# Wider output blocks, an early part of the second block, and a residual on one engine, in a two-layer decoder on one core

## The chip, the cores and the metric

One Trainium2 chip (trn2), one NeuronCore of it. The metric is the device time of one execution in microseconds (us), the lower the better. The engines go by the names of the profile: PE is TensorE (matrix products), DVE VectorE, ACT ScalarE, POOL GpSimd, SP SyncE, whose queue issues the weight loads.

## What is computed

Two layers of a decoder over 256 positions of width 2048, in float32. Each layer has three parts, each normalised before and after and added to the residual stream `h`:

```python
h = h + rms_norm(einsum('bsc,cd->bsd', mix, w_out[l]), mix_post_g[l])
xa = memory_attention(rms_norm(h, x_pre_g[l]), rms_norm(mem, mem_g[l]), x_wq[l], x_wkv[l], x_wo[l])
h = h + rms_norm(xa, x_post_g[l])
ff = swiglu(rms_norm(h, f_pre_g[l]), f_w_gu[l], f_w_down[l])
h = h + rms_norm(ff, f_post_g[l])
```

`mix` (2048 columns, 16 chunks of 128) joins three groups of heads: differential attention (chunks 0 to 5), a sparse attention (6 to 11) and a gated product along the positions (12 to 15). Their closing product is w_out. The cross-attention over 256 memory positions closes with x_wo (4 chunks), the feed-forward network (5632 hidden columns, in two halves of 22 chunks) with w_down.

## The kernel before

**Products.** A weight is used once. `loaded` fetches it on SP's queue into one of three `raw` tiles (128 x 2048, 1 MB), `splits` makes of each 1024 columns a rounded part `hi` (ACT, line 206) and the rest `lo` (DVE, line 207), and each chunk is used in three products: rounded by rounded, rounded by rest, rest by rounded. There are three `hi` and three `lo` tiles, so PE can be three tiles behind the split at most. Two loops use them. `mm_t` holds the weights and moves 256 positions of `x`. `mm_n` (line 399) holds 128 positions of its input and moves `cols` columns of the weights; its input goes by its tile's name in the rows, `mx` (the mix), `cx` (cross-attention) or `hx` (the hidden columns), so that `acc<-hi,hx` is a closing product of the feed-forward. Per chunk it makes two `hi` and one `lo` product for each of two row tiles. `acc` has four banks, and each call of `mm_n` takes two.

**The closing products.** `TAIL` (line 259) lists the column blocks of w_out, x_wo and both halves of w_down: three of 512 and two of 256. The first half's result is copied to `og`, the second half's added to it. `project_out` (line 648) empties each block: a square on ACT with a row sum (`sqj`), and the product with the gain, on DVE or, where the second half is added, on POOL (line 681). For the last block the gain's product is held back (`rest`).

**The order at w_out.** The first block takes its chunks in the order of `MIX_FIRST`: 8 to 11, 0 to 3, 6 and 7, then 4 and 5, 12 to 15. The generators `b_heads`, `a_heads` and `chunks` split the chunks of `mix` when they are there; the first eight lie in the tiles `m6`, as `mx` is not free yet (in orders of instructions these tiles are `m_` and a number). The chain that ends last is that of the third pair of heads: transposes `oat`, scaling (`MX`), split (`mx`) for chunks 4 and 5; and the gate: `yp` on PE, a sum on DVE (`y`), POOL's product into `MX`, split for 12 to 15. `turn_memory` waits for these and then fetches and splits the memory for the cross-attention.

**The residual.** `residual` (line 585) sums the squares, forms the row factor on DVE (`rs_v`, `rs_r`, ...), adds to `H`, transposes `H` (`xtp`) and splits it for the next products. Behind x_wo and at the change of layer nothing else is there for PE to do (`bare`), so 38 `warm` products stand in between. Behind w_out the product `t_k` (names `mh`, `ml`: memory) runs meanwhile; there the last eight chunks are added as `beside`: scaled on ACT (line 601) and added on POOL (line 602). `begin` fixes the order of DVE and ACT as written during the first steps; else the program's scheduler places the instructions. `last_residual` (line 689) ends the kernel: `hsum` adds three pieces on PE, DVE five, and each goes out by DMA.

Of the kernel before, what the change touches and what calls it, by code (L numbers as in the profile page):

```python
# [58 lines left out]
def trunk(ctx: ExitStack, tc, a, onehot, out):  # L59
# [17 lines left out]
    nc.gpsimd.memset(pc.tile([P, 8], F32, name="half_pc"), 0.0)  # L77
# [181 lines left out]
    TAIL = ((0, 512), (512, 512), (1024, 512), (1536, 256), (1792, 256))  # L259
    MIX_FIRST = ((8, 4), (0, 4), (6, 2), (4, 2), (12, 4))  # L260

    def plan():
# [7 lines left out]
        for l in range(L):  # L270
# [25 lines left out]
            for i, (c0, n) in enumerate(TAIL):  # L296
                yield spec(rows(w_out, c0, n), KD, n, MIX_FIRST if i == 0 else None)
# [101 lines left out]
    def mm_n(nk, cols, xh, xl, hold=False):  # L399

        xh, xl = ([x[:, k, :] for k in range(nk)] if not isinstance(x, list) else x for x in (xh, xl))
        tiles = [acc.tile([P, 512], F32, tag="acc", name="acc") for _ in range(2)]
        for n, k, hi, lo in weights(nk, cols, hold):
            for t in range(2):
                o = tiles[t][:, :cols]
                h, lw = xh[k][:, t * P:(t + 1) * P], xl[k][:, t * P:(t + 1) * P]
                mm(o, h, hi, n == 0, False)
                mm(o, h, lo, False, False)
                mm(o, lw, hi, False, n == nk - 1)
        return tiles  # L410
# [174 lines left out]
    def residual(og, ss, evac, nxt, res, bare, off):  # L585
# [11 lines left out]
        def add(c, n, beside=False):  # L597
            f = slice(c * P, (c + n) * P)
            for t in range(2):
                if beside:  # L600
                    nc.scalar.activation(og[:, t, f], og[:, t, f], AF.Copy, scale=r[:, t:t + 1])
                    nc.gpsimd.tensor_tensor(H[:, t, f], H[:, t, f], og[:, t, f], op=ALU.add)
                else:
                    nc.vector.scalar_tensor_tensor(H[:, t, f], og[:, t, f], r[:, t:t + 1], H[:, t, f],  # L604
                                                   op0=ALU.mult, op1=ALU.add)
# [3 lines left out]


# [6 lines left out]
        if bare:  # L617
            prefetch()
# [6 lines left out]
        add(8, 4, not bare)  # L625
# [4 lines left out]
        add(12, 4, not bare)  # L630
# [17 lines left out]
    def project_out(nk, xh, xl, og, gain, add=False, first=None):  # L648
# [4 lines left out]
        for g, (c0, cols) in enumerate(TAIL):  # L653
# [6 lines left out]
            tiles = mm_n(nk, cols, *(first if first and g == 0 else (xh, xl)), hold=last)  # L660

            def evac(tiles=tiles, g=g, c0=c0, cols=cols, gb=gb, last=last):
                for t in range(2):
                    d, p = og[:, t, c0:c0 + cols], tiles[t][:, :cols]
                    if add:
                        nc.vector.tensor_tensor(d, p, d, op=ALU.add)
                        square(d, ss[:, t, g:g + 1])
                        if not last:
                            nc.gpsimd.tensor_tensor(d, d, gb, op=ALU.mult)
                    else:  # L670
                        square(p, ss[:, t, g:g + 1])
                        if not last:
                            nc.vector.tensor_tensor(d, p, gb, op=ALU.mult)
                if not last:
                    return

                def rest():
                    for t in range(2):
                        d, p = og[:, t, c0:c0 + cols], tiles[t][:, :cols]
                        if add:  # L680
                            nc.gpsimd.tensor_tensor(d, d, gb, op=ALU.mult)
                        else:
                            nc.vector.tensor_tensor(d, p, gb, op=ALU.mult)
                return rest
# [4 lines left out]
    def last_residual(og, ss, evac):  # L689
# [599 lines left out]
```

## Time and profile before

| | us |
|---|---|
| median of three runs (lowest, highest) | 2424.31 (2423.04, 2426.93) |
| the profiled execution | 2425.12 |
| its span, first to last instruction | 2423.4 |
| PE busy | 2389.2 (99%) |
| DVE busy | 1412.6 (58%) |
| ACT busy | 1188.7 (49%) |
| POOL busy | 201.9 (8%) |
| weights and inputs read | 444.72 MB |

The mean granted clock of PE over the span is 0.997 of full. Where PE is busy nearly all the time, the shares of the others say little by themselves; what is to be read is what a product costs, and the few stretches where PE waits or its clock is lower.

### The profile page before, as it was taken

The numbers are of one execution on the slowest core, as the hardware profiler recorded it, in microseconds if no ns is written. First come the engines' busy times: TensorE is split into PE (matmuls) and PEld (weight loads), VectorE is DVE, ScalarE is ACT, GpSimd is POOL, SyncE is SP. The second block draws the span as 40 slices with busy tenths as digits, with TensorE's granted clock in tenths as the row PEclk, the third lists the DMA queues.
The fourth block names the chain that finished last, engine by engine and source line by source line (L and its number), as shares of the span: only waits on it lengthen the run. The fifth ranks groups of instructions, "written<-read, shape, count | busy, mean of one in ns | idle before, by whom it ended". The sixth has DMA issues, their size and how long they took to land.

```text
span 2423.4 us, 42616 instructions
## 1 busy us (share of the span) xinstructions
PE 2389.2 (99%) x17741; PEld 2249.2 (93%) x17741; DVE 1412.6 (58%) x2129; ACT 1188.7 (49%) x1764; POOL 201.9 (8%) x177
## 2 busy tenths in 40 slices
PE   9999999999999999999999999999999999999998
PEld 8899789999998999998999997999999989999987
DVE  5686766665554455555466767666655544555554
ACT  5655545554444444444455655455544444444443
POOL 0010131000000000000100102100000000000001
PEclk9999999999999999999999999999999999999999
DMA  7755475455655565555554555644555555555553
GB/s 250 242 170 157 164 252 176 157 176 196 197 195 194 187 195 193 192 192 192 190 173 132 187 156 189 219 157 157 190 194 192 191 192 190 192 195 196 193 191 131
DMA packets 356757, 453.27 MB, mean 187 GB/s; under 512 B 11290, under 2 KB 275412, under 8 KB 356052
## 3 DMA queue, kind: packets, MB, share of 16 engines
q1 hardware_dynamic: 354836, 443.45, 55.9%
q0 software_dynamic: 1248, 6.29, 0.8%
q8 instruction: 139, 2.28, 0.4%
q10 hardware_dynamic: 480, 0.80, 0.1%
q14 instruction: 54, 0.44, 0.1%
HBM read 444.72 MB, written 5.79 MB: 186 GB/s over the span
## 4 chain that ended last, share of the span: by engine, by line
PE 91%; DVE 4%; ACT 2%; DMA 2%; issue 1%; SPq 0%; POOL 0%; ACTq 0%; POOLq 0%; DVEq 0%
PE acc L201 86%; DVE lo L207 2%; ACT hi L206 1%; PE xtp L564 1%; PE ixp L201 1%; ACT sqj L550 1%; PE lga L201 1%; DMA m<-in_mem_dram 1%; DVE H L604 1%; DMA H<-in_x_dram 0%; DVE mx L207 0%; PE warm L416 0%; DMA lp<-in_a_lambda_dram 0%; PE pvb L201 0%; PE lgx L201 0%
## 5 line engine op out<-in xcount | busy, mean ns | idle before, releaser
L207 DVE TENSOR_TENSOR lo<-raw,hi 128x1024 fp32r<-128x1024 f32 (+2 forms) x839 | 1000.9, 1194 | 870.7 <-ACT hi L206 868.4
L206 ACT ACTIVATE hi<-raw 128x1024 fp32r<-128x1024 f32 (+2 forms) x839 | 861.0, 1027 | 1037.7 <-PE acc L201 954.7
L201 PE MATMUL acc<-x,hi 128*128 128x256 f32 (+1 forms) x7360 | 1270.0, 277 | 0.0
L201 PEld LDWEIGHTS acc<-x,hi 128*128 128x128 f32 (+1 forms) x7360 | 1111.2, 188 | 2.8 <-issue 2.7
L201 PE MATMUL acc<-x,lo 128*128 128x256 f32 x3680 | 889.5, 278 | 6.8 <-DVE lo L207 4.6
L201 PEld LDWEIGHTS acc<-x,lo 128*128 128x128 f32 x3680 | 690.1, 188 | 13.4 <-DVE lo L207 6.1
L201 PE MATMUL acc<-hi,hx 128*128 128x512 f32 (+1 forms) x1760 | 452.6, 347 | 0.0
L201 PEld LDWEIGHTS acc<-hi,hx 128*128 128x128 f32 x1760 | 308.5, 189 | 41.7 <-issue 0.2
L201 PE MATMUL acc<-lo,hx 128*128 128x512 f32 (+1 forms) x880 | 304.9, 347 | 0.0
L201 PEld LDWEIGHTS acc<-lo,hx 128*128 128x128 f32 x880 | 166.7, 189 | 20.5 <-issue 0.2
L1243 POOL TENSOR_TENSOR g<-g,u 128x512 f32<-128x512 f32 x44 | 76.6, 1741 | 1131.3 <-ACT g L1241 1131.3
L201 PE MATMUL acc<-hi,mx 128*128 128x512 f32 (+1 forms) x576 | 148.1, 345 | 7.9 <-DVE mx L207 4.0
L201 PEld LDWEIGHTS acc<-hi,mx 128*128 128x128 f32 x576 | 99.6, 190 | 21.8 <-DVE mx L207 5.1
L201 PE MATMUL acc<-hi,x 128*128 128x384 f32 (+1 forms) x384 | 109.3, 360 | 0.0
L201 PE MATMUL acc<-lo,mx 128*128 128x512 f32 (+1 forms) x288 | 98.4, 343 | 0.1
L201 PEld LDWEIGHTS acc<-hi,x 128*128 128x128 f32 x384 | 70.1, 188 | 8.3 <-issue 3.3
L201 PE MATMUL acc<-lo,x 128*128 128x384 f32 (+1 forms) x192 | 69.7, 363 | 0.0
L212 ACT ACTIVATE x<-xtp,gT 128x256 fp32r<-128x256 f32 x96 | 39.5, 470 | 48.7 <-PE xtp L564 48.7
L201 PEld LDWEIGHTS acc<-lo,mx 128*128 128x128 f32 x288 | 54.6, 190 | 7.0 <-DVE lo L207 1.0
L213 DVE SCALAR_TENSOR_TENSOR x<-xtp,gT,x 128x256 fp32r<-128x256 f32 x96 | 41.6, 478 | 16.1 <-ACT x L212 15.9
L201 PE MATMUL acc<-hi,cx 128*128 128x512 f32 (+1 forms) x160 | 42.7, 352 | 0.0
L201 PEld LDWEIGHTS acc<-lo,x 128*128 128x128 f32 x192 | 36.1, 188 | 3.9 <-issue 1.3
(247 smaller groups left out, 1878.4 us busy)
## 6 DMA issues: line engine op xcount, KB each, us to landing
raw<-in_f_w_gu_dram SPq DMA_DIRECT2D x352, 512.0 KB, 4.5
raw<-in_f_w_down_dram SPq DMA_DIRECT2D x76, 1024.0 KB, 5.1
raw<-in_w_out_dram SPq DMA_DIRECT2D x30, 1024.0 KB, 5.4
raw<-in_w_in_dram SPq DMA_DIRECT2D x48, 512.0 KB, 4.7
raw<-in_w_in_dram SPq DMA_DIRECT2D x23, 1024.0 KB, 5.3
raw<-in_x_wkv_dram SPq DMA_DIRECT2D x16, 1024.0 KB, 4.9
raw<-in_w_in_dram SPq DMA_DIRECT2D x12, 960.0 KB, 5.1
raw<-in_x_wq_dram SPq DMA_DIRECT2D x8, 1024.0 KB, 5.2
```

The lines of the kernel that those rows point to most:

```text
L201: return nc.tensor.matmul(o, lhsT=lhsT, rhs=rhs, start=start, stop=stop, skip_group_check=True)
L206: nc.scalar.activation(hi, src, AF.Copy)
L207: eng.tensor_tensor(lo, src, hi.bitcast(F32), op=ALU.subtract)
L212: nc.scalar.activation(hi, src, AF.Copy, scale=scale)
L213: nc.vector.scalar_tensor_tensor(lo, src, scale, hi.bitcast(F32), op0=ALU.mult, op1=ALU.subtract)
L550: nc.scalar.activation(q[:, :src.shape[-1]], src, AF.Square, accum_out=red)
L564: nc.tensor.transpose(p[:, t * P:(t + 1) * P], src[:, t, (c + j) * P:(c + j + 1) * P], ident)
L604: nc.vector.scalar_tensor_tensor(H[:, t, f], og[:, t, f], r[:, t:t + 1], H[:, t, f], op0=ALU.mult, op1=ALU.add)
L1243: nc.gpsimd.tensor_tensor(g, g, u, op=ALU.mult)
```

## The change

The blocks of `TAIL` become four of 512. The first two blocks of w_out are cut into an early part (ten chunks) and a late one (six): both early parts come first, then both late ones, each pair of `acc` banks kept in between (`more`, `into`). In a last block the last two chunks go tile by tile. The residual behind w_out makes all its additions on DVE, and `rest` is on DVE everywhere. `last_residual` gets 24 `warm` products between its two rounds of `hsum`, and the first half's closing product is followed by `warm(2)`. `turn_memory` starts one weight later. Two paddings move tiles: `cx` starts 64 bytes earlier, which puts it at 416 past a multiple of 512 bytes, as `hx` and `mx` are (it was at 480); the one in `pc` keeps the others where they were.

```diff
-    TAIL = ((0, 512), (512, 512), (1024, 512), (1536, 256), (1792, 256))
-    MIX_FIRST = ((8, 4), (0, 4), (6, 2), (4, 2), (12, 4))
+    TAIL = ((0, 512), (512, 512), (1024, 512), (1536, 512))
+
+    MIX_EARLY, MIX_LATE = ((8, 4), (0, 4), (6, 2)), ((4, 2), (12, 4))
...
+            for part, n in ((MIX_EARLY, 10), (MIX_LATE, 6)):
+                for c0, cols in TAIL[:2]:
+                    yield spec(rows(w_out, c0, cols), n, cols, part)
+            for c0, cols in TAIL[2:]:
+                yield spec(rows(w_out, c0, cols), KD, cols)
...
+    def mm_n(nk, cols, xh, xl, hold=False, into=None, more=False):
...
+        tiles = into or [acc.tile([P, 512], F32, tag="acc", name="acc") for _ in range(2)]
...
+        for w in weights(nk, cols, hold):
+            if hold and w[0] >= nk - 2:
+                end.append(w)
+                if w[0] < nk - 1:
+                    continue
+                for t in range(2):
+                    for w in end:
+                        step(t, *w)
...
+        if not bare:
+            add(0, 2)
+            turn(0)
+            add(2, 2)
+            rest()
+            yield
+            turn(2)
+            for c in range(4, KD, 2):
+                add(c, 2)
+                yield
+                turn(c)
+            yield
+            yield from pre_norm(res)
+            return
...
+                return lambda: [scaled(t, nc.vector) for t in range(2)]
...
+        warm(24)
         dg = spread(r)
-        rest()
...
-        at = used[0]
+        at = used[0] + 1
...
-            while used[0] == at or any(g.__name__ in ("last_heads", "chunks") for g in side):
+            while used[0] <= at or any(g.__name__ in ("last_heads", "chunks") for g in side):
...
+        early = [mm_n(10, cols, *first, more=True) for _, cols in TAIL[:2]]
+        oss, evac = project_out(KD, mxx[:, 0], mxx[:, 1], og, a["mix_post_g"][l], early=early)
...
-        cx = kp.tile([P, 2080], F32R, name="cx")[:, 32:].rearrange("p (a h t) -> p a h t", a=2, h=4)
+        cx = kp.tile([P, 2064], F32R, name="cx")[:, 16:].rearrange("p (a h t) -> p a h t", a=2, h=4)
...
+                warm(2)
```

The order on PE at the start of w_out, layer 0, as it was (from the last products of chunk 7 to the first of the `yp`):

```order
L201 MATMUL acc<-lo,mx 128x512
L201 MATMUL acc<-hi,mx 128x512
L1014 MATMUL oat<-ident,o_3079 128x128 x4
L201 MATMUL acc<-hi,mx 128x512
L201 MATMUL acc<-lo,mx 128x512
L201 MATMUL acc<-hi,mx 128x512
L201 MATMUL acc<-lo,mx 128x512
L201 MATMUL yp<-wsT,vg 128x128 x2
L201 MATMUL acc<-hi,mx 128x512 x3
L201 MATMUL acc<-lo,mx 128x512
L201 MATMUL acc<-hi,mx 128x512 x2
```

Behind the ten early chunks stood `oat`, and directly behind that the products that need its split. Now, from the same place:

```order
L201 MATMUL acc<-lo,mx 128x512
L201 MATMUL acc<-hi,mx 128x512
L201 MATMUL acc<-hi,m_2366 128x512 x2
L201 MATMUL acc<-lo,m_2366 128x512
L201 MATMUL acc<-hi,m_2366 128x512
L201 MATMUL acc<-lo,m_2366 128x512
L201 MATMUL acc<-hi,m_2366 128x512 x2
L201 MATMUL acc<-lo,m_2366 128x512
L201 MATMUL acc<-hi,m_2366 128x512 x2
L201 MATMUL acc<-lo,m_2366 128x512
L201 MATMUL acc<-hi,m_2366 128x512
L201 MATMUL acc<-hi,m_2367 128x512
L1040 MATMUL oat<-ident,o_3079 128x128 x4
```

and further on, where block 1's early part ends and the late part of block 0 begins:

```order
L201 MATMUL acc<-lo,m_2366 128x512
L201 MATMUL acc<-hi,m_2367 128x512
L201 MATMUL acc<-hi,mx 128x512
L201 MATMUL acc<-lo,mx 128x512
L201 MATMUL acc<-hi,mx 128x512 x2
L201 MATMUL yp<-wsT,vg 128x128 x4
L201 MATMUL acc<-lo,mx 128x512
L201 MATMUL acc<-hi,mx 128x512 x2
```

The tiles `m_` and `mx` of the early chunks are used a second time, for block 1: 60 products, with `oat` behind the 13th of them and four of the eight `yp` near their end; the other four `yp` stand four products into chunk 4.

On DVE, in the residual behind w_out of layer 0, it was:

```order
L472 SCALAR_TENSOR_TENSOR rs_u<-rs_q,rs_r 128x2
L473 SCALAR_TENSOR_TENSOR rs_r<-rs_u,rs_r 128x2
L604 SCALAR_TENSOR_TENSOR H<-og,rs_r,H 128x256 x8
L207 TENSOR_TENSOR lo<-raw,hi 128x1024 x2
L213 SCALAR_TENSOR_TENSOR x<-xtp,gT,x 128x256 x4
L207 TENSOR_TENSOR lo<-raw,hi 128x1024 x2
```

and it is now:

```order
L491 SCALAR_TENSOR_TENSOR rs_u<-rs_q,rs_r 128x2
L492 SCALAR_TENSOR_TENSOR rs_r<-rs_u,rs_r 128x2
L619 SCALAR_TENSOR_TENSOR H<-og,rs_r,H 128x256 x11
L207 TENSOR_TENSOR lo<-raw,hi 128x1024
L619 SCALAR_TENSOR_TENSOR H<-og,rs_r,H 128x256 x5
L207 TENSOR_TENSOR lo<-raw,hi 128x1024
L213 SCALAR_TENSOR_TENSOR x<-xtp,gT,x 128x256 x4
L207 TENSOR_TENSOR lo<-raw,hi 128x1024 x2
```

Eight additions of 256 columns stood ahead of the next `lo` tiles, the other half of the sum being on POOL; now there are eleven, one `lo`, and five more.

## Rows read from the trace of the kernel before

**Rows 1.** The page: engine totals (busy us, share, instructions), and the waits' chain by line

```profile
PE 2389.2 (99%) x17741; PEld 2249.2 (93%) x17741; DVE 1412.6 (58%) x2129; ACT 1188.7 (49%) x1764; POOL 201.9 (8%) x177
...
PE acc L201 86%; DVE lo L207 2%; ACT hi L206 1%; PE xtp L564 1%; PE ixp L201 1%; ACT sqj L550 1%; PE lga L201 1%; DMA m<-in_mem_dram 1%; DVE H L604 1%; DMA H<-in_x_dram 0%; DVE mx L207 0%; PE warm L416 0%; DMA lp<-in_a_lambda_dram 0%; PE pvb L201 0%; PE lgx L201 0%
```

**Rows 2.** PE by line and form: count | busy us, mean ns | idle before, releasers

```profile
L201 PE MATMUL acc<-hi,hx 128*128 128x256 f32 x704 | 127.4, 283 | 0.0
L201 PE MATMUL acc<-hi,mx 128*128 128x512 f32 x320 | 102.0, 395 | 7.9 <-DVE mx L207 4.0 <-ACT mx L206 3.9
L201 PE MATMUL acc<-hi,mx 128*128 128x256 f32 x256 | 46.4, 283 | 0.0
...
L201 PE MATMUL acc<-mh,lo 128*128 128x256 f32 x128 | 34.2, 297 | 5.4 <-DVE lo L207 5.4
L201 PE MATMUL acc<-hi,cx 128*128 128x512 f32 x96 | 31.8, 402 | 0.0
L201 PE MATMUL acc<-hi,cx 128*128 128x256 f32 x64 | 11.2, 276 | 0.0
...
L201 PE MATMUL yp<-wsT,vg 128*128 128x128 f32 x32 | 4.8, 284 | 0.6 <-DVE y L1088 0.6
```

**Rows 3.** Timeline, PE, w_down's second half, layer 0: start, us, instruction, count [idle before]

```profile
1177.58 0.39 PE L201 MATMUL acc<-lo,hx 128*128 128x512 f32 x1
...
1178.26 0.39 PE L201 MATMUL acc<-lo,hx 128*128 128x512 f32 x1
...
1180.95 0.28 PE L201 MATMUL acc<-lo,hx 128*128 128x256 f32 x1
...
1181.31 0.28 PE L201 MATMUL acc<-lo,hx 128*128 128x256 f32 x1
```

**Rows 4.** Timeline, PE, first block of w_out, layer 0

```profile
288.20 0.50 PE L201 MATMUL acc<-hi,mx 128*128 128x512 f32 x1 [1.95 <-ACT mx L206]
...
292.07 0.97 PE L201 MATMUL acc<-hi,mx 128*128 128x512 f32 x3 [2.04 <-DVE mx L207]
```

**Rows 5.** Timeline, POOL and DVE, the same stretch

```profile
287.69 3.78 POOL L1079 TENSOR_TENSOR vg<-vg,lnb 128x512 f32<-128x512 f32 x2 [122.60 <-ACT MX L1015]
...
288.04 2.31 DVE L207 TENSOR_TENSOR lo<-raw,hi 128x1024 fp32r<-128x1024 f32 x1
290.27 1.74 DVE L207 TENSOR_TENSOR mx<-MX,mx 128x512 fp32r<-128x512 f32 x1
```

**Rows 6.** Timeline: residual behind w_out, layer 0; last row, behind x_wo

```profile
378.55 7.40 DVE L604 SCALAR_TENSOR_TENSOR H<-og,rs_r,H 128x256 f32<-128x256 f32 x8
...
379.94 5.73 POOL L602 TENSOR_TENSOR H<-H,og 128x512 f32<-128x512 f32 x4 [3.60 <-ACT og L601]
...
387.23 0.55 PE L201 MATMUL acc<-mh,lo 128*128 128x256 f32 x1 [2.68 <-DVE lo L207]
...
481.59 1.67 DVE L604 SCALAR_TENSOR_TENSOR H<-og,rs_r,H 128x256 f32<-128x256 f32 x4
```

**Rows 7.** Windows: length, then busy (count) of PE, PEld, DVE, ACT, POOL; PEclk, DMA, GB/s

```profile
387.07:390.48 3.41, 3.25 (x15) 3.28 (x16) 3.41 (x7) 0.55 (x2) 0.00 (x0) 0.50 0.17 59
...
1585.15:1588.56 3.41, 2.83 (x13) 2.86 (x14) 3.41 (x7) 0.92 (x4) 0.00 (x0) 0.50 0.11 39
```

**Rows 8.** Timeline, PE: transposes behind x_wo (layer 0) and at the change of layer

```profile
482.78 1.03 PE L564 MATMUL xtp<-ident,H 128*128 128x128 f32 x8
...
1216.65 1.63 PE L564 MATMUL xtp<-ident,H 128*128 128x128 f32 x8 [0.88 <-DVE H L604]
```

**Rows 9.** The end: timeline of DVE and PE, and a window of the output's transfer

```profile
2414.69 3.40 DVE L708 SCALAR_TENSOR_TENSOR H<-og,rs_r,H 128x512 f32<-128x512 f32 x5
...
2414.92 4.34 PE L201 MATMUL hsum<-og,dg 128*128 128x512 f32 x6 [2.68 <-DVE dg L487]
...
2416.40:2421.80 5.40, 2.86 (x5) 0.86 (x3) 1.68 (x3) 1.79 (x3) 0.00 (x0) 0.82 1.01 382
```

**Rows 10.** The page: DMA issues, KB each, median us from issue to landing

```profile
raw<-in_w_out_dram SPq DMA_DIRECT2D x30, 1024.0 KB, 5.4
```

More of the change, by code (lines that the diff above doesn't have):

```diff
@@ L397, in mm_t, with step @@
         return tiles
-    def mm_n(nk, cols, xh, xl, hold=False):
+    def mm_n(nk, cols, xh, xl, hold=False, into=None, more=False):
         xh, xl = ([x[:, k, :] for k in range(nk)] if not isinstance(x, list) else x for x in (xh, xl))
[L402 to L409, printed above, removed]
+        tiles = into or [acc.tile([P, 512], F32, tag="acc", name="acc") for _ in range(2)]
+        def step(t, n, k, hi, lo):
+            o = tiles[t][:, :cols]
+            h, lw = xh[k][:, t * P:(t + 1) * P], xl[k][:, t * P:(t + 1) * P]
+            mm(o, h, hi, n == 0 and not into, False)
+            mm(o, h, lo, False, False)
+            mm(o, lw, hi, False, n == nk - 1 and not more)
+        end = []
+        for w in weights(nk, cols, hold):
[6 more added lines that the diff above has]
+                        step(t, *w)
+            else:
+                for t in range(2):
+                    step(t, *w)
         return tiles
@@ L624, in residual @@
         turn(6)
-        add(8, 4, not bare)
+        add(8, 4)
         yield
@@ L629, in residual @@
         turn(10)
-        add(12, 4, not bare)
+        add(12, 4)
         yield
@@ L646, in begin, with project_out @@
         start(gen)
-    def project_out(nk, xh, xl, og, gain, add=False, first=None):
+    def project_out(nk, xh, xl, og, gain, add=False, early=()):
         ss = sm.tile([P, 2, len(TAIL)], F32, tag="sso", name="sso", bufs=2)
@@ L659, in project_out, with scaled @@
                 nc.gpsimd.dma_start(gb, gain[c0:c0 + cols].partition_broadcast(P))
-            tiles = mm_n(nk, cols, *(first if first and g == 0 else (xh, xl)), hold=last)
+            if g < len(early):
+                tiles = mm_n(6, cols, [xh[:, k, :] for k in range(KD)], [xl[:, k, :] for k in range(KD)], into=early[g])
+            else:
+                tiles = mm_n(nk, cols, xh, xl, hold=last)
             def evac(tiles=tiles, g=g, c0=c0, cols=cols, gb=gb, last=last):
+                def scaled(t, eng):
+                    d, p = og[:, t, c0:c0 + cols], tiles[t][:, :cols]
+                    if add:
+                        eng.tensor_tensor(d, d, gb, op=ALU.mult)
+                    else:
+                        nc.vector.tensor_tensor(d, p, gb, op=ALU.mult)
                 for t in range(2):
@@ L666, in evac @@
                         nc.vector.tensor_tensor(d, p, d, op=ALU.add)
[L667 to L684, printed above, removed]
+                    square(d if add else p, ss[:, t, g:g + 1])
+                    if not last:
+                        scaled(t, nc.gpsimd)
+                return lambda: [scaled(t, nc.vector) for t in range(2)]
             if last:
@@ L703, in last_residual @@
             t, f = pieces[i]
+            if i == 2:
+                rest()
             p = summed.get((t, f.start))
```

18 lines of the change are left out of this document (5 added, 13 removed).

## Prediction

> **What bounds the kernel now.** I read the engine totals and the chain of waits first. TensorE is busy 99% of the span, and 86% of the chain that ended last is `acc` products of line 201 [rows 1]. So the time is a count of matmuls times their spacing, plus the few places where TensorE stands still or runs at half clock; work on other engines matters only there. I then grouped TensorE's rows by form (how many products of which width, and the idle time ahead of them, [rows 2]), took the spacing from a stretch where wide and narrow blocks meet [rows 3], and went to each place with idle time: the start of the output projection [rows 4, 5], the residual behind it [rows 6, 7], the change of layer [rows 8] and the end [rows 9].
>
> The reader is to see three things. Three products of 512 columns start 0.68 us apart from the next three (1177.58 to 1178.26), three of 256 columns 0.36 us (1180.95 to 1181.31): 0.2267 us against 0.1200 us each [rows 3], so that two narrow ones cost 0.0133 us more than the wide one that does the same work. At the start of w_out TensorE waits 1.95 and 2.04 us for the split of a late chunk [rows 4]. Behind w_out it waits for a `lo` tile, 5.4 us in both layers together [rows 2], and then the granted clock is at 0.50, the 1.2 GHz level, for 3.41 us in each layer [rows 7].
>
> The sum is made against the profiled execution (2425.1 us, a span of 2423.4 and 1.7 around it), which lies 0.8 us above the median of the three runs. What counts as no change is 0.2%, 4.8 us.
>
> **The change, part by part.**
>
> *Blocks of 512 in place of two of 256.* In w_down the narrow form with `hx` has 704 `hi` products [rows 2] and, by the loop (one `lo` for two `hi`), 352 `lo`: 1056, or 528 pairs, at 0.0133 us: -7.0 us over both halves and both layers. In w_out (`mx`) 256 + 128 = 384, or 192 pairs, -2.6 us; the mean of a narrow `mx` product is the same 283 ns as that of `hx` [rows 2]. The cross-attention's output (`cx`) is different: its narrow products are 7 ns shorter than the others (276 against 283), its wide ones 7 ns longer than those of `mx` (402 against 395) [rows 2], so widening alone would cost 48 pairs some +0.3 us. But the change also moves `cx` by 64 bytes, to the place within 512 bytes at which `hx` and `mx` lie; if its wide products then go like theirs, 144 of them save 7 ns, -1.0 us. I take -1.0 and keep +0.3. Ten chunks of the second block now come from the `m6` tiles: 120 wide products in two layers, between 0 and 7 ns dearer by the same rows, +0.4 taken. Sum -10.2 us, between -10.6 and -8.5. No cover is needed: these rows lie on the path. Narrow and wide blocks load the same bytes, in pieces twice as long, and split them in the same 1024-column tiles.
>
> By the Trainium skill (TensorE: Matmul & The Clock Gate, Back-to-back issue gap) a warm matmul takes N/2.4 ns plus about 2.5 ns; by that a pair would save 2.5 ns and not 13.3, and the whole part about 2 us. The measured rows differ from it, and the sum goes by the rows.
>
> *Early chunks of block 1 ahead of the late chunks of block 0.* Before, the chunks whose split comes last (4, 5 and 12 to 15) stand in the first block, directly behind the others. In the new order ten chunks of the second block, 60 products at 0.2267 = 13.6 us, come between; the transposes `oat` stand 13 products into them, which leaves 47, or 10.7 us, from there to the first product of chunk 4. The split that TensorE waited for, slowed while POOL worked, ended at 292.0 (290.27 + 1.74) [rows 5]; TensorE had run dry at 286.25 (288.20 - 1.95) [rows 4], directly behind `oat`. That is 5.8 us, and 10.7 us cover it. What goes: 7.9 us ahead of `hi,mx` and 0.6 us ahead of `yp`, both layers [rows 2], 8.5 us. What is late next: chunks 12 to 15, which need the `yp` product, the DVE add, POOL's multiply and a split, behind it. The second group of `yp` stands four products into chunk 4, with 20 products (4.5 us) from there to chunk 14; I count their chain at about 4 us. I leave 0.3 us of waiting per layer: -7.9 us, between -8.5 and -4.5 (where one of the two long waits per layer returns). All four `acc` banks are held in this time; block 2 opens behind the late chunks of block 1 (36 products, 8.2 us), which is the time that DVE and ACT have to empty block 0.
>
> *The residual behind w_out.* Before, eight adds on DVE take 7.40 us, 0.92 each, with POOL's adds beside them; the same adds alone take 1.67 us for four, 0.42 each [rows 6]. The next `lo` comes behind them, and TensorE waits 2.68 us for it [rows 6]. Now eleven adds stand there, then a `lo`, then five. With POOL empty, eleven take 4.6 us: 2.8 us less than the eight did, which is the length of the wait. Then come `lo` (1.2), five adds (2.1) and `lo`: 4.5 us for two tiles that feed TensorE for 2 x 24 products, over 5 us at 0.11 each. So TensorE keeps its feed with little to spare. The bounds for an add are 0.42 and 0.92 (both rows of this kernel); I take 0.42, since the only thing that differs between them is POOL. With the wait goes what followed it, 3.41 us at half clock per layer: half of the busy time there, 3.25 and 2.83 us [rows 7], 1.6 + 1.4 = 3.0 us. In all 5.4 + 3.0 = 8.4 us; I leave 0.6 us: -7.8 us, between -8.4 and -3. ACT loses four scalings and gains nothing here.
>
> *The change of layer.* Last product, 38 warming products, transposes. Behind the cross-attention the eight transposes take 1.03 us with no wait; at the change of layer 0.88 us of idle time stand ahead, and they take 1.63 us [rows 8]: 1.5 us more. Here a `lo` stood between the last two additions and POOL multiplied beside DVE's chain; both go, and the first tile is ready six products (1.4 us) earlier, while the last addition, square and multiply are twice as wide. The multiply by the gain on DVE (two operations of up to 0.7 us) falls behind the first adds, where DVE has gaps. -1.3 us, between -1.5 and 0. At the cross-attention the warming products cover the chain already: 0.
>
> *Two warming products behind the first half.* 2 x 0.12 us per layer, on the path: +0.5 us. Nothing waits there, so they buy nothing that I see.
>
> *The end.* The 24 warming products keep TensorE busy, so that `hsum` should run at full clock: its 4.34 us [rows 9] may become 2.6. But from 2416.4 to 2421.8 the DMA engines are full (share 1.01, 382 GB/s [rows 9]) with the 2.1 MB of output. What starts that stream is the first add on DVE at 2414.69 [rows 9], not `hsum`. The two gain multiplies go to DVE ahead of that add, and POOL is out of the way: one costs about 0.68 us (an add of 512 columns, 3.40 / 5 [rows 9]), the other saves about as much. 0, between -1 and +0.7.
>
> **Sum:** -10.2 - 7.9 - 7.8 - 1.3 + 0.5 + 0 = -26.7 us. From the median: 2424.3 - 26.7 = 2397.6 us.
>
> **The rivals.**
>
> 1. *The adds still starve TensorE.* Sixteen adds in one row on DVE leave two `lo` tiles late by as much as before, and the clock falls again. For it: DVE is busy all through the stretch, and the margin is a few tenths of a us. Against: 0.42 us alone. The 7.8 us are lost: 2405.4 us. At 0.92 each it would be worse (eleven adds 10.2 us, a wait of 5.4 us): 2411. Chance 0.13.
>
> 2. *Wide blocks win nothing.* For it: `cx`, where one wide product takes two narrow ones. Against: the direct rows of `hx` [rows 3]. All 10.2 us are lost: 2407.8 us. Chance 0.05. The rule of the Trainium skill (TensorE: Matmul & The Clock Gate) given above comes near this rival.
>
> 3. *The first wait only moves* (the change doesn't do what it says): chunks 12 to 15 come as late against their new place as chunk 4 did. For it: POOL's multiply and DVE's slowing lie in that chain [rows 5]. Against: 10.7 us of new cover. The 7.9 us are lost: 2405.5 us. Chance 0.07.
>
> 4. *Slower: w_out runs short of weights.* Cutting the first two blocks into early and late parts makes four half-full loads per layer, each of which holds one of three raw buffers. The stage uses 1 MB in 24 x 0.2267 = 5.44 us, and a load takes 5.4 us from issue to landing [rows 10]. If loads stopped overlapping, each would add the time until a buffer is free. From 1.0 us for each of 32 loads on (two layers, four blocks of four) 31.5 us are lost, and the kernel is slower by over 0.2%; at 1.4 us it would stand at 2442. For it: 5.4 beside 5.44. Against: three buffers, and TensorE waits for no load in this stage before, at the same use. Chance 0.03.
>
> **How the numbers follow.** The forecast has 0.70; rivals 1, 2 and 3 have 0.25 together, the slower one 0.03; 0.02 for a wait that eats the gain to within 0.2%. The forecast's own bounds are about 2393 (all terms at their best: -10.6 - 8.5 - 8.4 - 1.5 + 0.5 - 1 = -29.5, and a us for the runs) and 2403. The range reaches to the single losses of rivals 1 and 3 and leaves out rival 2, the worse form of 1, and two losses at once: 2393 to 2406. Faster 0.94 (also in rivals 1 to 3), same 0.03, slower 0.03.
>
> **What would show it.** In the changed profile: no narrow `hx`, `mx` or `cx` products, and wide ones 0.2267 us apart, `cx` included; under 1 us of idle time ahead of `hi,mx` and `yp`; adds of 0.42 us, no clock of 0.50 in the middle of the span, under 1 us of idle ahead of `mh,lo`; no idle time ahead of the transposes at the change of layer; `hsum` at full clock and the DMA engines as full as before, with the end no nearer. A clock at 0.50 behind the adds, or idle time of 2 us in the mix, would make the prediction wrong by 4 to 8 us; `cx` at its old spacing by 1.

## The result, and the profile after

| | before | changed kernel |
|---|---|---|
| median, us (lowest, highest of four) | 2424.39 (2423.04, 2426.93) | 2397.15 (2395.65, 2398.70) |
| profiled execution, us | 2425.12 | 2396.82 |
| its span, us | 2423.4 | 2395.1 |

The ratio is 0.9886, with a 95% interval from 0.9869 to 0.9904: 27.2 us faster, where 26.7 had been forecast. The two medians agree to half a us, but the terms do not agree that well one by one, and a good total can hide this. So the trace comes first.

The page of the changed kernel, its totals and its chain, against [rows 1]:

```profile
PE 2375.6 (99%) x17001; PEld 2210.7 (92%) x17001; DVE 1405.8 (59%) x2129; ACT 1182.5 (49%) x1720; POOL 183.5 (8%) x159
...
PE acc L201 89%; PE xtp L583 1%; DVE lo L207 1%; PE ixp L201 1%; PE lga L201 1%; PE warm L435 1%; DMA m<-in_mem_dram 1%; ACT hi L206 1%; ACT sqj L569 0%; DMA lp<-in_a_lambda_dram 0%; PE pva L201 0%; PE pvb L201 0%; PE ptp L443 0%; DMA H<-in_x_dram 0%; PE lgx L201 0%
```

PE is at 99% as before, with 740 products fewer. TensorE's products line by line and form by form (count | busy us, mean ns | idle before), against [rows 2]:

```profile
L201 PE MATMUL acc<-hi,hx 128*128 128x512 f32 x1408 | 434.1, 389 | 0.0
...
L201 PE MATMUL acc<-hi,mx 128*128 128x512 f32 x384 | 120.7, 391 | 0.0
...
L201 PE MATMUL acc<-hi,cx 128*128 128x512 f32 x128 | 41.2, 395 | 0.0
...
L201 PE MATMUL acc<-mh,lo 128*128 128x256 f32 x128 | 32.1, 283 | 0.0
...
L201 PE MATMUL yp<-wsT,vg 128*128 128x128 f32 x32 | 4.8, 274 | 0.0
```

No narrow `hx`, `mx` or `cx` product is left. The idle time ahead of `hi,mx`, `yp` and `mh,lo` was 7.9, 0.6 and 5.4 us and is 0.0 in all three.

The residual behind w_out, layer 0: first the timeline of DVE, then a window over PE, PEld, DVE, ACT, POOL (busy, count), clock, DMA share, GB/s; against [rows 6, 7]:

```profile
373.13 4.44 DVE L619 SCALAR_TENSOR_TENSOR H<-og,rs_r,H 128x256 f32<-128x256 f32 x11
...
378.63 2.06 DVE L619 SCALAR_TENSOR_TENSOR H<-og,rs_r,H 128x256 f32<-128x256 f32 x5
...
372.00:383.00 11.00, 11.00 (x97) 11.00 (x97) 10.89 (x27) 9.46 (x22) 0.00 (x0) 1.00 0.34 102
```

Eleven additions take 4.44 us, 0.40 each, POOL does nothing, PE is busy for all of the 11 us at a clock of 1.00.

The end, as timelines of DVE and PE and one window of the output's transfer, against [rows 9]:

```profile
2386.35 3.39 DVE L734 SCALAR_TENSOR_TENSOR H<-og,rs_r,H 128x512 f32<-128x512 f32 x5
...
2386.58 2.81 PE L201 MATMUL hsum<-og,dg 128*128 128x512 f32 x6 [0.86 <-DVE dg L506]
...
2387.90:2393.30 5.40, 1.50 (x4) 0.38 (x2) 1.85 (x3) 1.61 (x3) 0.00 (x0) 1.00 0.99 373
```

`hsum` is faster by 1.5 us, and from the first addition to the end of the span it takes 8.75 us (2395.1 - 2386.35), where it took 8.71 (2423.4 - 2414.69).

The starts of each stage's first products give the lengths of the stages in the two traces:

| stage | before, us | after, us | difference | forecast |
|---|---|---|---|---|
| first warming products to the first `x` product | 5.84 | 7.96 | +2.1 | 0 |
| w_out, layers 0 and 1 | 101.26, 97.29 | 94.01, 90.71 | -13.8 | -10.1 |
| `t_k`, layers 0 and 1 | 29.38, 29.34 | 24.91, 24.92 | -8.9 | -7.8 |
| x_wo, both layers | 23.97 each | 23.55, 23.54 | -0.9 | -1.0 |
| first three halves of w_down | 121.45 each | 119.70 each | -5.3 | -5.3 |
| two warming products, both layers | - | 0.23 each | +0.5 | +0.5 |
| the change of layer | 6.96 | 6.05 | -0.9 | -1.3 |
| last half of w_down to the end | 135.33 | 134.76 | -0.6 | -1.8 |
| all others | | | -0.5 | 0 |
| span | 2423.4 | 2395.1 | -28.3 | -26.7 |

The first three halves of w_down came out to the tenth. Waits at w_out were worth some 2.5 to 3 us more than their idle time; the end lost 1.2 us that the wide blocks won there; and the start differs by 2.1 us, which the change doesn't touch: in the fourteen profiles of this study the first `lo` product on `x` starts between 8.6 and 11.6 us. Two single times are therefore not to be compared within some 3 us, but stages are, to 0.5 us.

### The profile page after: what moved, and what is told of

The parts are those of the page before. It is cut to its first block, busy times and chain, and to the rows that moved or that the text cites. A ratio compares the mean times of both kernels' runs of the same rounds, so it can differ in the third digit from the quotient of the medians.

```text
span 2395.1 us, 41059 instructions
## 1 busy us (share of the span) xinstructions
PE 2375.6 (99%) x17001; PEld 2210.7 (92%) x17001; DVE 1405.8 (59%) x2129; ACT 1182.5 (49%) x1720; POOL 183.5 (8%) x159
## 4 chain that ended last, share of the span: by engine, by line
PE 94%; DMA 2%; DVE 2%; ACT 1%; issue 0%; SPq 0%; POOL 0%; ACTq 0%; POOLq 0%
PE acc L201 89%; PE xtp L583 1%; DVE lo L207 1%; PE ixp L201 1%; PE lga L201 1%; PE warm L435 1%; DMA m<-in_mem_dram 1%; ACT hi L206 1%; ACT sqj L569 0%; DMA lp<-in_a_lambda_dram 0%; PE pva L201 0%; PE pvb L201 0%; PE ptp L443 0%; DMA H<-in_x_dram 0%; PE lgx L201 0%
## 5 line engine op out<-in xcount | busy, mean ns | idle before, releaser
L201 PEld LDWEIGHTS acc<-x,lo 128*128 128x128 f32 x3680 | 690.6, 188 | 13.8 <-DVE lo L207 6.2
L201 PE MATMUL acc<-hi,hx 128*128 128x512 f32 x1408 | 434.1, 389 | 0.0
L201 PEld LDWEIGHTS acc<-hi,hx 128*128 128x128 f32 x1408 | 264.3, 188 | 54.9 <-issue 0.2
L201 PE MATMUL acc<-lo,hx 128*128 128x512 f32 x704 | 274.3, 390 | 0.0
L201 PEld LDWEIGHTS acc<-lo,hx 128*128 128x128 f32 x704 | 132.2, 188 | 27.5 <-issue 0.2
L201 PE MATMUL acc<-hi,mx 128*128 128x512 f32 x384 | 120.7, 391 | 0.0
L201 PEld LDWEIGHTS acc<-hi,mx 128*128 128x128 f32 x384 | 71.9, 188 | 14.9 <-DVE mx L207 0.2
L201 PE MATMUL acc<-lo,mx 128*128 128x512 f32 x192 | 75.0, 391 | 0.0
L213 DVE SCALAR_TENSOR_TENSOR x<-xtp,gT,x 128x256 fp32r<-128x256 f32 x96 | 41.4, 477 | 15.6 <-ACT x L212 15.3
L201 PEld LDWEIGHTS acc<-lo,mx 128*128 128x128 f32 x192 | 36.1, 188 | 7.3
L201 PE MATMUL acc<-hi,m 128*128 128x512 f32 x128 | 41.8, 398 | 0.0
L201 PE MATMUL acc<-hi,cx 128*128 128x512 f32 x128 | 41.2, 395 | 0.0
```

The source lines that it names most:

```text
L201: return nc.tensor.matmul(o, lhsT=lhsT, rhs=rhs, start=start, stop=stop, skip_group_check=True)
L213: nc.vector.scalar_tensor_tensor(lo, src, scale, hi.bitcast(F32), op0=ALU.mult, op1=ALU.subtract)
```

## Experiments

**The width alone.** `TAIL` as it was, everything else as changed (a padding keeps the tiles' places):

```diff
-    TAIL = ((0, 512), (512, 512), (1024, 512), (1536, 512))
+    TAIL = ((0, 512), (512, 512), (1024, 512), (1536, 256), (1792, 256))
```

> The changed kernel with its last block of 512 cut into two of 256 again, in all closing products, and nothing else undone (the padding in front keeps the tiles' places). Theory: two narrow products cost 0.0133 us more than a wide one. Each half of w_down takes 121.45 us again in place of 119.70, each w_out 1.3 us more, x_wo about 0.3 us more (now that cx lies like the others, a narrow cx product should take 0.120 and not 0.113): 7.0 + 2.6 + 0.6 = +10.2 us, about 2407. Rival: width alone wins little (2.5 ns a pair, +2 us, 2399) and w_down got shorter by something else in the change, so that its stages stay at 119.7 to 120.0.

Measured: 2407.03 us (2404.42 to 2408.59), +9.9. Three of the halves of w_down take 121.45, 121.44 and 121.45 us again; w_out takes 1.5 and 1.3 us more, x_wo 0.3 us each: 8.6 us in all, and the rival of 2.5 ns a pair is out. The last half did not grow: from its start to the end it takes 134.66 us, against 134.76 with wide blocks. Its last product starts 0.9 us later (122.17 us into the stage, and not 121.24: 1.75 of spacing, less a `hsum<-H` piece of 0.86 us that here stands behind it), but the first addition of the residual follows 3.90 us behind that and not 4.76, as the work of DVE and ACT on a narrow last block is shorter. The narrow `cx` products, by form:

```profile
L201 PE MATMUL acc<-hi,cx 128*128 128x256 f32 x64 | 11.8, 283 | 0.0
```

At the new place a narrow `cx` takes 283 ns like all others, and not 276 as in [rows 2]. The `t_k` stage also grew, by 1.6 and 1.7 us, and the stage behind it got 1.0 us shorter each time, as eight transposes now stand in `t_k`. The rest is a wait: 1.3 us of idle time return ahead of `mh,lo`, 0.67 in each layer. The timeline of DVE, layer 0, shows why:

```profile
370.87 6.03 DVE L619 SCALAR_TENSOR_TENSOR H<-og,rs_r,H 128x256 f32<-128x256 f32 x15
376.81 1.21 DVE L207 TENSOR_TENSOR lo<-raw,hi 128x1024 fp32r<-128x1024 f32 x1
```

The edit changed the scheduler's order too: fifteen additions stand ahead of the `lo` here, and not eleven. So +9.9 is not the width's spacing alone; 1.4 us of it are this order. And the residual's gain rests on that order.

**One early part.** Block 1 runs whole behind block 0, whose late chunks again stand directly behind its early ones:

```diff
-                for c0, cols in TAIL[:2]:
+                for c0, cols in TAIL[:1]:
...
-            for c0, cols in TAIL[2:]:
+            for c0, cols in TAIL[1:]:
...
-        early = [mm_n(10, cols, *first, more=True) for _, cols in TAIL[:2]]
+        early = [mm_n(10, cols, *first, more=True) for _, cols in TAIL[:1]]
```

> The changed kernel with only block 0 of w_out cut into early and late chunks, so that the late chunks of block 0 stand directly behind its early ones, as before; block 1 runs whole behind it. Theory: the waits for chunks 4 and 5 and the gate come back, with idle time of about 4.2 us ahead of hi,mx and yp in each layer, and each w_out stage grows by about 5.2 us (94.0 to 99.2, 90.7 to 95.9), since a stop costs a little more than the idle time that the profile shows: +10.4 us, about 2407.6. Rival a: a stop costs its idle time only, +4.2 us per layer, +8.4. Rival b: other parts of the change (the later memory) had already taken the waits away, then under +2 us.

Measured: 2410.04 us (2408.07 to 2412.22), +12.9; the stages grow by 5.8 and 7.2 us. The waits are back: by form, then a window of layer 1.

```profile
L201 PE MATMUL acc<-hi,mx 128*128 128x512 f32 x448 | 142.7, 396 | 7.6 <-ACT mx L206 3.9 <-DVE mx L207 3.7
...
L201 PE MATMUL yp<-wsT,vg 128*128 128x128 f32 x32 | 5.6, 316 | 0.5 <-DVE y L1114 0.5
```

```profile
1482.66:1489.49 6.83, 5.13 (x16) 4.06 (x15) 2.53 (x3) 0.52 (x1) 1.89 (x1) 0.50 0.46 154
```

8.1 us of idle time return, but the stages grow by 13.0. Two things make the difference. In layer 1 the granted clock fell to 0.50 (1.2 GHz) for 6.83 us after the first stop; in the kernel before, it had not fallen there. And in layer 0, without such a fall, 4.3 us of idle time (1.95, 2.04 and 0.29) cost 5.8: each stop costs something beyond it. The starts of the products show where. The last `oat` ahead of the first stop starts at 286.61 us, 0.11 behind the one before it; the profile counts it as busy until 286.88. Over the four places with idle time in this stage some 0.65 us lie in such ends. Most of the rest lies behind the stops: behind the first two, the first product starts 0.33 us ahead of the second one (288.83 to 289.17), where dense ones are 0.23 apart. Why was not looked into. Both rivals of the expectation are out (+8.4, and under +2), and so is the forecast's third: without the early part of block 1 the waits stand where they were, and with it they are gone, not moved.

**The old residual.** Eight additions on DVE, the other half scaled on ACT and added on POOL:

```diff
+        def beside(c, n):
+            f = slice(c * P, (c + n) * P)
+            for t in range(2):
+                nc.scalar.activation(og[:, t, f], og[:, t, f], AF.Copy, scale=r[:, t:t + 1])
+                nc.gpsimd.tensor_tensor(H[:, t, f], H[:, t, f], og[:, t, f], op=ALU.add)
...
+            beside(8, 4)
...
+            beside(12, 4)
```

> The changed kernel with the old residual behind w_out: half the additions on DVE, half scaled on ACT and added on POOL. Theory: DVE's eight adds take 0.92 us each again, the lo tile is late, TensorE waits 2.7 us and runs 3.4 us at half clock in each layer; the t_k stage takes 29.3 us in place of 24.9: +8.9 us, about 2406. Rival: the wait went because the last block of w_out is wide or ends tile by tile (DVE starts the residual with more lo tiles ahead), then the stage stays at 25 to 26 us and the time within 2 us of 2397.

Measured: 2405.73 us (2403.48 to 2406.05), +8.6. `t_k` takes 27.96 and 29.59 us, 3.1 and 4.7 more. On DVE (timeline, layer 0), and by form on PE:

```profile
374.07 6.40 DVE L619 SCALAR_TENSOR_TENSOR H<-og,rs_r,H 128x256 f32<-128x256 f32 x8
```

```profile
L201 PE MATMUL acc<-mh,lo 128*128 128x256 f32 x128 | 33.9, 294 | 4.7 <-DVE lo L207 4.7
```

Eight additions take 6.40 us, 0.80 each, and `mh,lo` waits for 4.7 us, 2.36 in each layer. In layer 0 the granted clock stayed at 1.00 behind the wait, in layer 1 it fell to 0.50 for 3.4 us; the 1.6 us between the two stages are what half clock costs here.

**POOL's work alone.** Seven operations that nothing needs, behind the row factor:

```diff
+        def spin(r):
+            nc.gpsimd.tensor_scalar(vX[:, 0, :], gX[:, 0:512], r[:, 0:1], None, op0=ALU.mult)
+            for _ in range(6):
+                nc.gpsimd.tensor_tensor(vX[:, 1, :], vX[:, 0, :], gX[:, 1024:1536], op=ALU.mult)
...
         if not bare:
+            spin(r)
             add(0, 2)
```

> The changed kernel with seven useless operations on POOL in the residual behind w_out (a product with the row factor, then six of 512 columns into a tile that is filled later), which nothing waits for. The result is the same. Theory: POOL's work is what slowed DVE's adds. With POOL busy for 8 us or more the sixteen adds take up to 0.92 us each in place of 0.42, the first eleven up to 10 us, and TensorE waits for lo: the t_k stage grows from 24.9 us to 29 to 33, with a clock of 0.50 behind it, the time by 8 to 16 us. Rival: the adds were slow because ACT read and wrote the same og tile, or because of their order; then they stay at 0.42 us and the time at 2397.

Measured: 2412.41 us (2412.31 and 2412.51), +15.3. The timelines of DVE, POOL and PE in layer 0, and a window behind the wait:

```profile
372.42 11.07 DVE L619 SCALAR_TENSOR_TENSOR H<-og,rs_r,H 128x256 f32<-128x256 f32 x11
...
374.42 8.38 POOL L1174 TENSOR_TENSOR vX<-vX,gX 128x512 f32<-128x512 f32 x6
...
384.77 0.55 PE L201 MATMUL acc<-mh,lo 128*128 128x256 f32 x1 [5.95 <-DVE lo L207]
```

```profile
384.77:387.90 3.13, 3.13 (x15) 3.13 (x16) 3.13 (x7) 1.45 (x4) 0.00 (x0) 0.50 0.00 0
```

The same eleven additions in the same order take 11.07 us in place of 4.44: 1.01 us each against 0.40. DVE waits for nothing of POOL's here, so it is POOL's running that slows DVE. TensorE waits 5.95 us in each layer, and its granted clock falls to 0.50. This has the size of the forecast's worse form of the first rival (5.4 us).

The mean hides two kinds of additions. The six beside POOL's six products of two tiles, and for comparison the eleven of the changed kernel (min/median/max in ns):

```profile
L619 DVE SCALAR_TENSOR_TENSOR H<-og,rs_r,H x6: 1485/1498/1546, 374.5 to 381.6; 128x256 f32<-128x256 f32 x6
```

```profile
L619 DVE SCALAR_TENSOR_TENSOR H<-og,rs_r,H x11: 479/480/486, 373.1 to 377.1; 128x256 f32<-128x256 f32 x11
```

Beside such a product an addition takes three times as long, and one addition gets through per product of POOL's (1.30 to 1.36 us each). Of the four additions beside POOL's first operation, which reads one tile, three took 0.48 us and one 0.92. The kernel before shows the same two kinds: its first four additions take 0.48 us each, and the four beside POOL's 1.49 to 1.54.

The Trainium skill (GPSIMD Engine Reference, Specifications) says that POOL shares its SBUF interfaces with DVE and names instructions with two SBUF inputs, which these additions are. The run agrees; the size, a factor of three while such a product runs, is this run's.

**The place of cx.** The old padding, the order of all instructions unchanged:

```diff
-        cx = kp.tile([P, 2064], F32R, name="cx")[:, 16:].rearrange("p (a h t) -> p a h t", a=2, h=4)
+        cx = kp.tile([P, 2080], F32R, name="cx")[:, 32:].rearrange("p (a h t) -> p a h t", a=2, h=4)
```

> The changed kernel with cx back at 480 past a multiple of 512 bytes (the old padding of 32 floats); the order of instructions is the same on every engine. Theory: the place sets the spacing of wide cx products, 0.2333 us instead of 0.2267, so that x_wo takes 96 x 0.0067 = 0.64 us more in each layer, 24.2 us in place of 23.55, and nothing else changes. Rival: the wide products with cx are at 0.2267 whatever its place (the old 7 ns came from the shape of the loop), 23.55 us.

x_wo takes 24.12 us in both layers, +0.57 (the whole, one execution: 2399.48). From the timeline of PE, layer 0, two neighbouring `lo` products, with two `hi` products between them:

```profile
460.19 0.39 PE L201 MATMUL acc<-lo,cx 128*128 128x512 f32 x1
...
460.89 0.39 PE L201 MATMUL acc<-lo,cx 128*128 128x512 f32 x1
```

and in the changed kernel:

```profile
460.13 0.39 PE L201 MATMUL acc<-lo,cx 128*128 128x512 f32 x1
...
460.81 0.39 PE L201 MATMUL acc<-lo,cx 128*128 128x512 f32 x1
```

0.70 us for three against 0.68: where `cx`, the held operand, starts within 512 bytes changes the spacing. Only these two places were tried, and why it does was not looked into.

**The end without its warming products.** `warm(24)` taken out of `last_residual`.

> The changed kernel without the 24 warming products at the end. Theory: the output's transfer bounds the end, so hsum at half clock (4.3 us in place of 2.8) costs 0 to 0.3 us from the first add on DVE to the end of the span (8.75 us in the changed kernel). Rival: the end follows the last hsum piece, then it takes about 1.5 us more, 10.2 us.

The end, as timelines of DVE and PE:

```profile
2384.81 3.40 DVE L733 SCALAR_TENSOR_TENSOR H<-og,rs_r,H 128x512 f32<-128x512 f32 x5
...
2385.04 4.51 PE L201 MATMUL hsum<-og,dg 128*128 128x512 f32 x6 [3.74 <-DVE dg L506]
```

`hsum` takes 4.51 us in place of 2.81, as the granted clock falls to 0.50 within it, and the span ends 8.8 us behind the first addition (2393.6 - 2384.81), as with the 24 products. They buy nothing, and the end does not follow the last `hsum` piece; the output's transfer, which fills the DMA engines (share 0.92 from 2386.0 to 2391.4 us), is what is left to set it.

**The end in order.** `hsum<-H` held behind the last closing product, and the gain's multiplies behind the first three additions:

```diff
-            mm(p, ident, H[:, t, f], True, False)
+            tc.keep_in_program_order(mm(p, ident, H[:, t, f], True, False))
...
-            last_residual(og, oss, evac)
+            with tc.manual_schedule(engines={DVE}):
+                last_residual(og, oss, evac)
```

> The changed kernel with two things of the end put in order: the three products hsum<-H behind the last closing product (the scheduler had put two of the three ahead of it), and the gain's two multiplies on DVE behind the first three additions and not ahead of the row factor. Theory: the first takes 0.87 us off the path, the second lets the first addition start 0.5 us earlier after the last product, and the transfer follows: 1.2 to 1.4 us less from the start of the last w_down to the end of the span. Rival: the multiplies now stand between the additions and starve the transfer for 0.7 us or more, or the stream has a fixed length and start, then 0.9 us less or nothing.

From the start of the last w_down to the end: 133.00 us in place of 134.76, -1.8. The last closing product starts 1.8 us earlier in the stage, where 0.9 was expected: each `hsum<-H` piece is two products of 0.43 us, and two pieces moved. The first addition follows it by 4.29 us and not 4.76. But 0.5 us were lost behind that: `hsum<-og` now queued behind 24 warming products, 1.39 us after the first addition (0.23 in the changed kernel), DVE's last two pieces went out 1.2 us later, behind the multiplies, and the transfer ran short.

**A version meant to be better.** The above, no `warm(2)`, 34 in place of 38 warming products, and at the change of layer one `lo` tile less ahead of the last additions.

> The end in the order of the run before this one, and three more edits: no two warming products behind the first half (-0.46 us; the order of all else stays), 34 in place of 38 warming products at the bare residuals (the transposes behind x_wo could start 0.5 us earlier: -0.5 us or nothing per layer, as what bounds may be the second pair of additions), and at the change of layer one lo tile less ahead of the last block's additions on DVE (-0.5 us, or a wait for lo behind the transposes in place of it). Theory: 2.5 to 3.5 us less than the changed kernel, about 2394. Rival: the shorter cover leaves the gaps where they were, then -1.7 us, 2395.5; or a lo tile comes late, then 2397.

Measured: 2411.76 us (2410.89 to 2412.81), 14.6 slower than the changed kernel. Of the other edits, the shorter cover behind x_wo gave what was hoped for (5.13 us in place of 5.61), and the change of layer less (5.86 for 6.05, where 0.5 was expected). What was lost: the second half's `x` products, 2112 in a row, took 248.75 us in each layer in place of 239.39, with no idle time in it. In the forecast I had priced the two warming products at +0.5 us and written that they buy nothing that I see. Three runs followed.

**The two warming products.** Out; then one; then three:

```diff
-                warm(2)
```

> The changed kernel without the two warming products behind the first half's closing product; the order of all other instructions is the same. New theory, from the run before: 256-column products that follow directly on the wide ones keep a spacing of 0.1178 us until something comes between, and two products with another weight and another moving tile are such a thing. Then the second half's gate and up stage of 2112 products takes 248.75 us in place of 239.39 in each layer and nothing else changes: 2 x 9.36 - 0.46 = +18.3 us, about 2415.4. Rival: the 9.4 us of that run come from one of its other edits (34 warming products, one lo tile less ahead, the order at the end); then this run is 0.5 us faster than the changed kernel, 2396.7.

> The changed kernel with one warming product in place of two at that point. If any product in between resets the spacing, the stage stays at 239.4 us and the kernel is 0.2 us faster than with two; if it takes a second narrow product of the same kind (a switch of weight and then none), the stage takes 248.8 us and the time is 18 us longer.

> The changed kernel with three warming products in place of two at the same point; the order of all else stays. One such product left the slow spacing of 0.1178 us, two gave 0.1133. If it takes a certain length of narrow products on tiles of their own, three do as well as two: the second half's stage at 239.4 us, the time 0.2 us above the changed kernel. If it is a matter of phase, that a certain offset between loads and products is hit by chance, three may miss it as one did: 248.8 us, and 18 us longer.

Measured: none 2414.48 us (2413.09 to 2417.34); one 2415.01 and three 2397.11, a single execution each. The second half's stage takes 248.75, 248.75 and 239.39 us. In the middle of it, one window of the same 100 us, without them:

```profile
890.00:990.00 100.00, 100.00 (x851) 100.00 (x851) 50.45 (x47) 42.34 (x44) 7.05 (x4) 1.00 0.56 184
```

with one:

```profile
890.00:990.00 100.00, 100.00 (x851) 100.00 (x851) 51.56 (x48) 41.27 (x43) 7.01 (x4) 1.00 0.57 189
```

with three:

```profile
890.00:990.00 100.00, 100.00 (x885) 100.00 (x884) 52.34 (x49) 43.51 (x45) 7.04 (x4) 1.00 0.61 196
```

and in the changed kernel, with two:

```profile
890.00:990.00 100.00, 100.00 (x885) 100.00 (x884) 52.30 (x49) 43.50 (x45) 7.04 (x4) 1.00 0.59 196
```

PE is 100% busy at full clock in all four, yet 851 products fit in one case and 885 in the other. Products of 256 columns that follow directly on wide ones start 0.1178 us apart (248.75 / 2112), and they stay so for a quarter of a ms. With two or three products in between they start 0.1133 us apart. Before the change the closing product ended in narrow blocks, and the stage took 239.38 us.

The same can be seen in a second place. In the changed kernel `t_k` follows wide blocks too, and nothing stands in between; before, it followed narrow ones. One window of 8 us each, changed kernel and before:

```profile
367.40:375.40 8.00, 8.00 (x70) 8.00 (x70) 7.05 (x22) 4.62 (x8) 0.54 (x1) 1.00 0.66 219
```

```profile
373.00:381.00 8.00, 8.00 (x73) 8.00 (x72) 7.09 (x21) 5.09 (x9) 1.60 (x2) 1.00 0.77 241
```

The first 76 products of `t_k` start 0.1178 us apart, until the transposes `xtp` come in between (0.1133 before): some 0.3 us per layer, not won yet. But wide products are not the only way into the slow spacing. In the kernel before, products of the same form on `x` run at both, 0.1178 us from 403.5 us on, behind transposes, and 0.1133 from 411.6 us on, behind four products `bc` of 128 columns:

```profile
403.50:410.50 7.00, 7.00 (x62) 7.00 (x61) 5.18 (x12) 3.16 (x6) 0.00 (x0) 1.00 0.62 215
411.60:418.60 7.00, 7.00 (x64) 7.00 (x63) 2.81 (x3) 3.31 (x4) 0.00 (x0) 1.00 0.53 174
```

So a dense run of these products keeps one of two spacings until something else stands in between. What decides which one it gets stays open.

**Again, with the two back.** The version above with `warm(2)`, and 14 warming products at the end:

> The run that was meant to be better, with the two warming products back and 14 in place of 24 at the end, so that hsum<-og doesn't queue behind them. Theory: 0.48 us less per layer at x_wo and 0.2 less at the change of layer, as in that run; at the end 0.87 us off the path, 0.47 from the earlier first addition, and the transfer no longer starved: 2.3 to 2.7 us less than the changed kernel at the same start, about 2394.7. Rival: the transfer is still held up by the multiplies between the additions, then 1.9 us less, 2395.3. The first stretch, up to the first weights, has varied by 2.5 us from run to run, so the stages are to be compared, not the two times alone.

Measured: 2393.47 us (2392.65 to 2395.26), ratio to the kernel before 0.9869 (0.9854 to 0.9884). By stages, against the changed kernel: 0.48 us less behind each x_wo, 0.19 at the change of layer, 2.1 from the last w_down to the end (132.69 us): 3.2 in all, more than the 2.3 to 2.7 expected, since the `hsum<-H` pieces were worth 1.8 us and not 0.9. The end, timelines of DVE and PE:

```profile
2384.59 2.07 DVE L734 SCALAR_TENSOR_TENSOR H<-og,rs_r,H 128x512 f32<-128x512 f32 x3
...
2384.82 2.81 PE L201 MATMUL hsum<-og,dg 128*128 128x512 f32 x6
...
2386.58 1.29 DVE L697 TENSOR_TENSOR og<-og,gF 128x512 f32<-128x512 f32 x2
```

`hsum` starts 0.23 us behind the first addition again, and ACT's pieces feed the transfer while DVE multiplies.

## Why the prediction was right, and where it was not

*Blocks of 512.* The mechanism and the spacing were right: w_down won 1.75 us in each of three halves, to the hundredth as forecast, and counting products in [rows 2] with the spacing from a stretch where both widths meet [rows 3] needed no assumption. That +9.9 us were measured against -10.2 when the width was undone is in part luck: 8.6 us of it are spacing, 1.4 the order of the residual's additions, and the last half, where 1.75 had been forecast, gave nothing in that comparison, since the chain behind a wide last block is longer. By the Trainium skill (TensorE: Matmul & The Clock Gate, Back-to-back issue gap) a pair saves 2.5 ns; that section gives its rule for a single product, and not for a stream with a weight load each. The run does not bear it out, and it would have made this part five times too small. `cx`: -1.0 forecast for both layers; x_wo lost 0.85, and moving `cx` back cost 1.1.

*Early chunks.* The mechanism was right and the size too small. I took the idle time in the profile, 8.5 us, as what a wait costs and left 0.6 of it. All of it went, and the w_out stages fell by 13.8 us, some 11 of it for the waits. The run that put the waits back shows why: 8.1 us of idle time cost 13.0, in part through the clock, in part at the stop itself and in the products right behind it.

*The residual.* Right: -7.8 forecast, -8.9 in the two stages; the old residual put 7.7 of it back (8.6 by the medians). I had left 0.6 us of waiting, and none was left. That POOL was the cause was only argued, from 0.92 against 0.42 us [rows 6]; the run with useless work on POOL shows it. The 0.92 was a mean that I took for one addition: four of the eight ran ahead of POOL's start at 0.40, and four beside it at 1.43 from start to start. That the additions moved to DVE do not starve TensorE rests on their speed with POOL idle and, as the run with the narrow last block shows, on how many of them the scheduler puts ahead of the `lo`, which I had not said.

*The change of layer.* -1.3 forecast, -0.9 measured. The 0.88 us of idle time went. What did not come is the rest of the 1.5 us: the transposes take as long as before (1.63 us in [rows 8]), each pair 0.40 us behind the last, which is the pace of the additions that feed them:

```profile
1202.19 1.62 PE L583 MATMUL xtp<-ident,H 128*128 128x128 f32 x8
```

The step that failed: I wrote that the `lo` between the last two additions goes. It does, but a `lo` now stands ahead of both, and the chain did not get short enough to be covered. With one less, the stage fell by a further 0.2 us only, together with four warming products less.

*The warming products.* The charge, +0.5 us, was right; "nothing waits there, so they buy nothing that I see" was wrong. They keep 18 us by the stages (2 x 9.36 - 0.46). In the trace before, narrow blocks stand at this place, so no row of it shows the loss; but both spacings of this product stand in it (403.5 and 411.6 us), and I had not looked for them. I took a place without a wait as a place where an instruction can do nothing, and that step failed.

*The end.* Forecast 0, between -1 and +0.7; measured +1.2 against what the wide blocks won in the last half. That the transfer bounds it was right, and `hsum` at half clock costs nothing. What I missed is that the scheduler puts two of the three `hsum<-H` pieces ahead of the last closing product, on the path, where one had stood before: 0.9 us more. And the first addition comes 0.3 us later behind the last product (4.76 us, not 4.45): with the multiplies moved from ahead of the row factor to behind three additions it comes after 4.29.

So it is partly luck that the total was right to half a us. By the two profiles, waits at w_out and in `t_k` were worth 4.8 us more than forecast; the end and the change of layer took 1.6 of that back, and a late start, which the change doesn't touch, 2.1: 28.3 us by the spans of the profiles, 27.2 by the medians.

## What to carry to other kernels

Where TensorE is busy all the time, count products by form and take their spacing from the trace, in the very place; 100% busy says nothing on how many fit in, and the same product ran at 0.1133 and 0.1178 us here for a quarter of a ms, depending on what stood ahead of it. An experiment that undoes one part can move the scheduler's order elsewhere, so compare it stage by stage. Before taking out an instruction that seems idle, measure the stage behind it. And before giving work to POOL to relieve DVE, look at what DVE does meanwhile: the work moved cost DVE more than it saved.

## What was not expected of the hardware

- A dense run of narrow products (256 columns) with another weight each time keeps 0.1178 or 0.1133 us per product, 2112 of them in a row. Directly behind wide products (512 columns) it was 0.1178, in `t_k` of the changed kernel and in the second half without its warming products; there two or three of these in between gave 0.1133, one did not. Behind transposes 0.1178 is seen too. Why was not found: a phase between weight loads and products would fit, but no run here shows it.
- The start of `cx`, the held operand, within 512 bytes (480 against 416) changes a wide product by 7 ns (0.70 against 0.68 us for three) and a narrow one by 7 ns the other way (276 against 283 ns).
- A stop of TensorE costs more than the idle time that the profile shows: 4.3 us of it made a stage 5.8 us longer at full clock.
- Beside POOL's products of two tiles an addition on DVE takes 1.5 us in place of 0.48, though it waits for nothing of POOL's: one gets through per product of POOL's.
